# Computing the first head group's values, queries and keys side by side in a two-layer hybrid trunk

## The chip, the cores and the metric

The kernel runs on one core of one Trainium2 chip. The metric is the device time in microseconds (us) of the whole program, taken over several executions. One execution is profiled; its trace gives the start and length of the instructions on each engine: TensorE (PE) for matmuls, VectorE (DVE), ScalarE (ACT), GpSimd (POOL) and SyncE (SP), which issues DMAs here.

## What is computed

A trunk of two layers over 256 positions and a model width of 2048, all in float32. Each layer is

```python
h = _rmsnorm(x, attn_norm[l])
z = jnp.einsum('bsd,dc->bsc', h, w_in[l])
(fq, fk, fv, fg, mq, mk, mv, dq, dk, dv, sq, sk, sv) = _split_cols(z)
fox = _forgetting_attention(...)       # gate fg + b_fgate, cumulative log-sigmoid
moba = _moba_attention(...)            # rotary positions on q and k
diff = _differential_attention(...)    # rotary, difference of two softmaxes, norm
sb = _stick_breaking_attention(...)    # log-sigmoid of scores, cumulated from the right
mixed = jnp.concatenate([...], axis=-1)
x = x + jnp.einsum('bsc,cd->bsd', mixed, w_out[l])
h = _rmsnorm(x, ffn_norm[l])
act = jax.nn.silu(h @ w_gate[l]) * (h @ w_up[l])
x = x + act @ w_down[l]
```

with four heads of 128 in each of the four groups (a product of one group and one of q, k, v is 2048 x 512), a feed-forward width of 5632, and a last RMSNorm. The `rmsnorm` is applied late: products are taken of x times the norm's gain, and the factor of each row (`rcol`) is multiplied in when a product is read out of PSUM.

## The kernel before

**Blocks.** All weights stream from memory as blocks of 128 x 1024 floats (512 KB). An "in" product (2048 x 512) is 8 blocks, each with two chunks of 128 rows. A layer has 96 "in" blocks, then 32 "out", 176 "ffn" and 88 "down" blocks; layer 1 begins at block 392. `ORDER` is diff, moba, sb, fox. `load` (L186) issues a block's DMA on SP's queue into one of four buffers (`raw`). `split_parts` rounds it on ACT to `hi` (L195) and takes the rest on DVE as `lo` (L196), three buffers of each. `rows_block` does the block's 12 matmuls of 128 x 512 on PE (L356 to L358: hi with x's lo, lo with x's hi, hi with x's hi, for two chunks and two halves of the positions). x is likewise kept in halves `xh` (L299 on ACT, L300 on DVE), 16 chunks.

**Order.** All engines work through queues in the order in which the program writes the instructions. `rows_block(b)` first calls `run_ahead(b)`, which splits block b+2 and issues loads up to block b+5, then writes the matmuls of b, then calls `tick`, which lets three queues of generators do one step each: `evacs` (reading products out of PSUM and turning them), `background` (the steps of attention of a group, after its q and k are ready) and `spare` (the gate of fox). A step's instructions so stand between the work of one block and the next. `drain(evacs)` does all that is left of that queue at once. The buffers of `hi` are such that hi of block n waits for PE's end of block n-3.

**Products.** Each "in" product has two PSUM tiles of the pool's tag "mm", which has four; small pieces take the four of the tag "at". Rotary products are read by four multiplies on DVE (`z` and `ms`, L415), two sums, two transposes (L384); `mem` is written by a DMA (L387) and read back by four (L393). Products without rotary are read by two copies on ACT (L425 for q and k, L815 for v).

**The start.** In layer 0, x comes two chunks with each of blocks 1 to 7, ahead of the block's load (`beside`); its chunks are squared on ACT, added on POOL, and `attn_norm_steps` makes `rcol` from the sum: a table load and Ln, a table load and Exp on ACT (L305, L306), four small operations on DVE (L307 to L310). In layer 1, x's chunks come out of the last down products (`add_turned`), four at a time.

**The first group.** diff has v, then q, then k, each 8 blocks; the other groups q, k, v. The gate's steps (`gate_steps`, spare) wait for 50 ticks of the layer, then do one step a tick: 32 sums `gacc` (L518 on DVE, half of them on POOL) and 16 small matmuls `pf` (L530) that stand ahead of block 84. Stick-breaking's chain: scores, exponentials, a table load and Ln on ACT (L707, L708), `n` on DVE (L711 to L715), its halves `h` on ACT (L720) and `l` on DVE (L721), and the updates of its scores on PE.

Of the kernel before, what the change touches and what calls it, by code (L numbers as in the profile page):

```python
# [11 lines left out]
F32 = mybir.dt.float32  # L12
# [7 lines left out]
P = 128  # L20
# [7 lines left out]
NJ = D // P  # L28
FFN = 5632
NF = FFN // P  # L30
GC = 512
# [6 lines left out]
ORDER = ("diff", "moba", "sb", "fox")  # L38
# [12 lines left out]
def columns(name, which):  # L51


    c0 = COL0[name] + "qkv".index(which) * GW
    order = np.arange(GW)
    if which != "v":
        order = order.reshape(NH, 4, 32).transpose(1, 0, 2).reshape(-1)
    return c0 + order
# [9 lines left out]
C_KEEP = C_SL + P  # L68
# [36 lines left out]
def lay_out(inp):  # L105

    pd, pf = turned(D), turned(FFN)
    x_t = np.ascontiguousarray(inp["x"][0].T[pd].reshape(NJ, P, S).transpose(1, 0, 2))
    vec = np.zeros((P, V_ALL), np.float32)
    blocks = np.empty((sum(n for _, _, n in plan()), P, 1024), np.float32)  # L110
    at = 0

    def put(w, rows, cols, wide):
        nonlocal at
        m = w[rows][:, cols] if not isinstance(cols, slice) else w[rows, cols]
        k = 1024 // wide
        nb = m.shape[0] // (k * P)
        blocks[at:at + nb] = m.reshape(nb, k, P, wide).transpose(0, 2, 1, 3).reshape(nb, P, 1024)
        at += nb

    for l in range(DEPTH):
        w_in, every = inp["w_in"][l][pd], slice(None)
        v = vec[:, l * V_LAYER:(l + 1) * V_LAYER]
        v[:, V_GA:V_GA + 16] = inp["attn_norm"][l][pd].reshape(16, P).T
        v[:, V_GF:V_GF + 16] = inp["ffn_norm"][l][pd].reshape(16, P).T
        v[:, V_WF:V_WF + 64] = w_in[:, FG0:FG0 + NH].reshape(16, P, NH).transpose(1, 0, 2).reshape(P, 64)
        v[:, V_SUB] = inp["diff_subln"][l]
        v[:, V_B:V_B + NH] = inp["b_fgate"][l]
        for n, name in enumerate(("diff_lq1", "diff_lk1", "diff_lq2", "diff_lk2")):
            v[:, V_LAM + 64 * n:V_LAM + 64 * (n + 1)] = inp[name][l]  # L130
        for kind, what, nb in plan():
            if what[0] != l:
                continue
            if kind == "in":
                put(w_in, every, columns(*what[1:]), GC)
            elif kind == "out":
                order = np.concatenate([HEAD0[g] * P + np.arange(GW) for g in ORDER])
                put(inp["w_out"][l], order[what[2] * 256:what[2] * 256 + 256], np.arange(what[1] * GC, what[1] * GC + GC), GC)
            elif kind == "ffn":
                c = slice(what[1] * GC, what[1] * GC + GC)  # L140
                for n, name in enumerate(("w_gate", "w_up")):
                    blocks[at:at + NJ, :, n * GC:n * GC + GC] = inp[name][l][:, c][pd].reshape(NJ, P, GC)
                at += NJ
            else:
                put(inp["w_down"][l], pf, slice(what[1] * GC, what[1] * GC + GC), GC)
    fin = np.ascontiguousarray(np.broadcast_to(inp["final_norm"], (P, D)))
    return {"x_t": x_t, "vec": vec, "w": blocks, "consts": constants(), "fin": fin}
# [7 lines left out]
def plan():  # L155

    out = []
    for l in range(DEPTH):
        for g in ORDER:
            out += [("in", (l, g, which), 8) for which in ("vqk" if g == ORDER[0] else "qkv")]  # L160
        out += [("out", (l, c, kb), 1) for c, kb in OUT_ORDER]
        out += [("ffn", (l, c), NJ) for c in range(NFC)]
        out += [("down", (l, c), NFC * 2) for c in range(4)]
    return out
# [3 lines left out]
def trunk(ctx: ExitStack, tc: tile.TileContext, x_t, vec, w, consts, fin, y):  # L168
# [39 lines left out]
    con = cp.tile([P, C_KEEP], F32, name="con")  # L208
    con_in = big.tile([P, C_ALL - C_KEEP], F32, name="con_in", tag="t13")
    nc.scalar.dma_start(vecs[:, :V_GF], vec[:, :V_GF])  # L210
    beside = {b: [(x_all[:, 2 * b:2 * b + 2], x_t[:, 2 * b:2 * b + 2])] for b in range(1, NJ // 2)}
    for b, (to, of, c0, c1) in enumerate([(con, consts, C_ID, C_KEEP), (con, consts, 1024, C_ID), (con, consts, 0, 1024),
                                          (vecs, vec, V_GF, V_ALL)]):
        beside[NJ // 2 + b] = [(to[:, c0:c1], of[:, c0:c1])]
    beside[NJ // 2 + 4] = [(con_in, consts[:, C_KEEP:])]
    raws[0] = wp.tile([P, 1024], F32, name="raw0", tag="raw", bufs=RAW)
    for j in range(2):
        nc.sync.dma_start(xs[j], x_t[:, j])
# [3 lines left out]
    def run_ahead(b):  # L222
        nonlocal loaded, done_split
        while done_split < min(b + SPLIT, n_blocks):
            while loaded < min(done_split + RAW, n_blocks):
                for to, of in beside.get(loaded, ()):
                    nc.sync.dma_start(to, of)
                load(loaded)
                loaded += 1
            if done_split < NJ // 2:  # L230
                parts = split_parts(done_split, 1 if done_split else 2)
                for j in range(2 * done_split, 2 * done_split + 2):
                    halves_of_x(j, vcol(0, V_GA + j))
                    next(parts, None)
                for _ in parts:
                    pass
            else:
                split(done_split)
            done_split += 1
# [38 lines left out]
    def drain(queue):  # L278
        while queue:
            step(queue)  # L280
# [461 lines left out]
    STEPS = {"fox": fox_steps, "moba": moba_steps, "diff": diff_steps, "sb": sb_steps}  # L742

    def setup_steps():
        while loaded < 16:
            yield
        V.tensor_copy(id_bf, ident)
        V.tensor_copy(mq_bf, con_in[:, C_MQ - C_KEEP:C_MQ - C_KEEP + P])
        V.tensor_copy(mk_bf, con_in[:, C_MK - C_KEEP:C_MK - C_KEEP + P])
        A.activation(con_r[:, :3], con_in[:, :3 * P].rearrange("p (n c) -> p n c", n=3), AF.Copy)  # L750
        A.activation(one_r, cst(C_ONE), AF.Copy)
        yield
        e = tp.tile([P, DEPTH, 2], F32, name="le", tag="le", bufs=1)
        for l in range(DEPTH):
            lv = vcol(l, V_LAM, 256).rearrange("p (a b d) -> p a b d", a=2, b=2)
            pr = tp.tile([P, 2, 64], F32, name="pr", tag="pr", bufs=1)
            V.tensor_tensor(pr, lv[:, :, 0], lv[:, :, 1], op=ALU.mult)
            V.tensor_reduce(e[:, l], pr, axis=AX, op=ALU.add)
        yield
        A.activation(e, e, AF.Exp)  # L760
        yield
        for l in range(DEPTH):
            init = 0.8 - 0.6 * math.exp(-0.3 * l)
            nl = cp.tile([P, 1], F32, name=f"nlam{l}")
            V.tensor_tensor(nl, e[:, l, 1:2], e[:, l, 0:1], op=ALU.subtract)
            V.tensor_scalar(nl, nl, -init, None, op0=ALU.add)
            state["nlam", l] = nl
            gs = cp.tile([P, 1], F32, name=f"gsub{l}")
            V.tensor_scalar(gs, vcol(l, V_SUB), 1.0 - init, None, op0=ALU.mult)
            state["gsub", l] = gs  # L770
        yield

    def first_squares():
        for j in range(NJ):
            square_sum(j)
            if j % 2:
                yield

    def attention(l):
        if l == 0:  # L780
            evacs.append(first_squares())
        evacs.append(attn_norm_steps(l))
        for n, name in enumerate(ORDER):
            at = 3 * (n % 2)
            qk = {which: tmp(at + i, [P, NH, S], which) for i, which in enumerate("qk")}
            vt = tmp(at + 2, [P, 2, GW], "v")
            ready = {}

            def v_part():
                outs = in_product()  # L790
                if n:
                    drain(evacs)
                evacs.append(v_steps(vt, outs, ready))
                if n:
                    drain(evacs)

            def pairs():
                for which in "qk":
                    evacs.append(q_or_k_steps(name, which, in_product(), qk[which], ready))

            if n == 0:
                if l == 0:
                    background.append(setup_steps())
                spare.append(gate_steps(l))
                v_part()
                pairs()
                background.append(group_steps(l, name, qk, ready))
            else:
                pairs()
                background.append(group_steps(l, name, qk, ready))  # L810
                v_part()

    def v_steps(vt, outs, ready):
        for t in range(2):
            A.activation(vt[:, t], outs[t], AF.Copy, scale=state["rcol"][:, t:t + 1])  # L815
        ready["v"] = vt
        yield
# [189 lines left out]
```

## Time and profile before

| | before |
|---|---|
| median of 3 runs | 2247.93 us (2247.28 to 2248.83) |
| the profiled execution | 2248.83 us |
| its span, first to last instruction | 2247.0 us |
| PE busy | 2223.6 us (99%) |
| DVE busy | 1301.0 us (58%) |
| ACT busy | 1054.6 us (47%) |
| POOL busy | 195.8 us (9%) |
| DMA, mean over the span | 212 GB/s |

A row of a timeline gives the start in us from the span's start, the time of the row's instructions, engine, line, operation, the tiles written and read with their shape, and how many followed one another (x2: the time is that of both). In brackets stand the engine's idle time just before and the instruction that ended it. The granted clock of PE is 1.00 at 2.4 GHz and 0.5 at 1.2 GHz; a table by windows gives its mean in each. Matmuls are pipelined: a row's time is longer than the step to the next one.

### The profile page before, as it was taken

The page shows a single profiled execution, that of the slowest core. Times are in us where ns is not written, and L with a number is a line of the kernel's source. Part 1 is how long each engine was busy: PE and PEld are TensorE (multiplying, and loading weights), DVE is VectorE, ACT ScalarE, POOL GpSimd, SP SyncE. Part 2 cuts the span into 40 slices and gives each one's busy share as a digit, 9 for nine tenths or more (in the row PEclk, how much of TensorE's full clock was granted, in tenths as well). Part 3 has the DMA queues.
Part 4 walks back from the last instruction along what each step waited for, and adds up shares of the span by engine and source line. Part 5 has one row for each costly group of instructions (what it writes and reads, how often), then busy time and mean ns, then how long its engine had stood idle before and what let it go on. Part 6 is the DMA issues. An engine that isn't in the chain of part 4 may idle for free.

```text
span 2247.0 us, 26619 instructions
## 1 busy us (share of the span) xinstructions
PE 2223.6 (99%) x9977; PEld 1832.2 (82%) x9977; DVE 1301.0 (58%) x1442; ACT 1054.6 (47%) x1296; POOL 195.8 (9%) x189
## 2 busy tenths in 40 slices
PE   9999999999999999999999999999999999999997
PEld 6888888788888888888878888878888888888886
DVE  6768655655555555455566776566555555554444
ACT  6454644544444444444444556445444444444443
POOL 2019200100000000000000290011000000000000
PEclk9999999999999999999999999999999999999999
DMA  7766556777667667666657565567777776676664
GB/s 256 225 206 203 181 188 206 231 223 216 215 217 227 209 212 226 213 207 206 209 196 232 191 203 188 183 214 228 226 223 237 250 231 211 224 223 199 201 196 147
DMA packets 190497, 476.42 MB, mean 212 GB/s; under 512 B 17440, under 2 KB 72992, under 8 KB 190368
## 3 DMA queue, kind: packets, MB, share of 16 engines
q1 hardware_dynamic: 189792, 473.93, 66.2%
q8 instruction: 78, 1.28, 0.2%
q10 hardware_dynamic: 576, 0.79, 0.1%
q14 instruction: 51, 0.42, 0.1%
HBM read 444.24 MB, written 30.41 MB: 211 GB/s over the span
## 4 chain that ended last, share of the span: by engine, by line
PE 89%; DMA 4%; DVE 3%; ACT 2%; issue 1%; SPq 1%; ACTq 0%; DVEq 0%
PE gate L374 20%; PE up L374 20%; PE po L356 9%; PE po L358 9%; PE po L357 9%; PE in L356 7%; PE in L357 7%; PE in L358 7%; DMA back<-mem 2%; DMA mem<-tr 2%; DVE lo L196 1%; ACT hi L195 1%; SPq L393 0%; DVE x_all L833 0%; DVE tr L384 0%
## 5 line engine op out<-in xcount | busy, mean ns | idle before, releaser
L196 DVE TENSOR_TENSOR lo<-raw,hi 128x1024 fp32r<-128x1024 f32 (+1 forms) x785 | 961.2, 1227 | 880.1 <-ACT hi L195 879.6
L195 ACT ACTIVATE hi<-raw 128x1024 fp32r<-128x1024 f32 (+1 forms) x785 | 829.6, 1059 | 1080.3 <-PE up L374 487.4
L374 PE MATMUL gate<-hi,xh 128*128 128x512 f32 x1408 | 548.2, 389 | 0.5 <-ACT hi L195 0.5
L374 PE MATMUL up<-hi,xh 128*128 128x512 f32 x1408 | 547.8, 389 | 0.0
L374 PEld LDWEIGHTS gate<-hi,xh 128*128 128x128 f32 x1408 | 264.3, 188 | 56.0 <-ACT hi L195 1.2
L374 PEld LDWEIGHTS up<-hi,xh 128*128 128x128 f32 x1408 | 264.4, 188 | 54.8
L356 PE MATMUL in<-hi,xh 128*128 128x512 f32 x768 | 304.7, 397 | 4.1 <-ACT hi L195 2.3
L357 PE MATMUL in<-lo,xh 128*128 128x512 f32 x768 | 301.5, 393 | 1.4 <-DVE lo L196 1.3
L358 PE MATMUL in<-hi,xh 128*128 128x512 f32 x768 | 301.0, 392 | 0.0
L374 PE MATMUL gate<-lo,xh 128*128 128x512 f32 x704 | 274.5, 390 | 1.1 <-DVE lo L196 1.1
L374 PE MATMUL up<-lo,xh 128*128 128x512 f32 x704 | 273.9, 389 | 0.0
L356 PE MATMUL po<-hi,act 128*128 128x512 f32 x704 | 273.9, 389 | 0.0
L357 PE MATMUL po<-lo,act 128*128 128x512 f32 x704 | 273.9, 389 | 0.0
L358 PE MATMUL po<-hi,act 128*128 128x512 f32 x704 | 273.9, 389 | 0.0
L356 PEld LDWEIGHTS in<-hi,xh 128*128 128x128 f32 x768 | 145.4, 189 | 34.9 <-ACT hi L195 3.4
L357 PEld LDWEIGHTS in<-lo,xh 128*128 128x128 f32 x768 | 145.3, 189 | 32.5 <-DVE lo L196 3.3
L358 PEld LDWEIGHTS in<-hi,xh 128*128 128x128 f32 x768 | 145.3, 189 | 30.7
L374 PEld LDWEIGHTS gate<-lo,xh 128*128 128x128 f32 x704 | 132.1, 188 | 30.6 <-DVE lo L196 3.4
L358 PEld LDWEIGHTS po<-hi,act 128*128 128x128 f32 x704 | 132.2, 188 | 27.5
L357 PEld LDWEIGHTS po<-lo,act 128*128 128x128 f32 x704 | 132.2, 188 | 27.4
L356 PEld LDWEIGHTS po<-hi,act 128*128 128x128 f32 x704 | 132.2, 188 | 27.4
L374 PEld LDWEIGHTS up<-lo,xh 128*128 128x128 f32 x704 | 132.2, 188 | 27.2
(206 smaller groups left out, 1473.8 us busy)
## 6 DMA issues: line engine op xcount, KB each, us to landing
raw<-w SPq DMA_DIRECT2D x783, 512.0 KB, 4.3
mem<-tr SPq DMA_DIRECT2D x50, 512.0 KB, 4.3
back<-mem SPq DMA_DIRECT2D x168, 128.0 KB, 4.8
k<-mem SPq DMA_DIRECT2D x24, 128.0 KB, 4.2
memb<-trb SPq DMA_DIRECT2D x16, 128.0 KB, 3.8
x_all<-memb SPq DMA_DIRECT2D x4, 512.0 KB, 6.2
x_all<-x_t SPq DMA_DIRECT2D x7, 256.0 KB, 7.1
q<-mem SPq DMA_DIRECT2D x8, 128.0 KB, 4.7
```

The source lines that it names most:

```text
L195: A.activation(hi[:, c], raw[:, c], AF.Copy)
L196: V.tensor_tensor(lo[:, c], raw[:, c], hi[:, c].bitcast(F32), op=ALU.subtract)
L356: T.matmul(outs[t], xlo, wh, start=first, stop=False)
L357: T.matmul(outs[t], xhi, wl, start=False, stop=False)
L358: T.matmul(outs[t], xhi, wh, start=False, stop=last)
L374: T.matmul(outs[n][t], st, wt[:, n * GC:(n + 1) * GC], start=first, stop=last)
```

## The change

The weights of diff are laid out so that blocks come in the order v, q, k of the first two chunks of x, then v, q, k of the next two, and so on ("first"). `attention` opens all three products at once, k's on two PSUM tiles of the tag "at", and runs through the 24 blocks; then it drains `evacs`, reads v out, and queues the steps for q and k. This holds for both layers. In layer 0 the pairs of x's chunks are loaded, halved and squared with every third block in place of every block, the constants with blocks 4, 7, 10 and 13, `con_in` with 16, and the setup waits for 20 loads.

```diff
@@ plan
         for g in ORDER:
-            out += [("in", (l, g, which), 8) for which in ("vqk" if g == ORDER[0] else "qkv")]
+            if g == ORDER[0]:
+                out += [("first", (l, g, which, kb), 1) for kb in range(8) for which in "vqk"]
+            else:
+                out += [("in", (l, g, which), 8) for which in "qkv"]
@@ trunk
-    beside = {b: [(x_all[:, 2 * b:2 * b + 2], x_t[:, 2 * b:2 * b + 2])] for b in range(1, NJ // 2)}
+    beside = {3 * p: [(x_all[:, 2 * p:2 * p + 2], x_t[:, 2 * p:2 * p + 2])] for p in range(1, NJ // 2)}
...
-        beside[NJ // 2 + b] = [(to[:, c0:c1], of[:, c0:c1])]
-    beside[NJ // 2 + 4] = [(con_in, consts[:, C_KEEP:])]
+        beside[4 + 3 * b] = [(to[:, c0:c1], of[:, c0:c1])]
+    beside[16] = [(con_in, consts[:, C_KEEP:])]
@@ run_ahead
-            if done_split < NJ // 2:
+            if done_split < 3 * NJ // 2 and done_split % 3 == 0:
                 parts = split_parts(done_split, 1 if done_split else 2)
-                for j in range(2 * done_split, 2 * done_split + 2):
+                p = 2 * done_split // 3
+                for j in range(p, p + 2):
@@ setup_steps
-        while loaded < 16:
+        while loaded < 20:
@@ first_squares
-            if j % 2:
-                yield
+            if j % 2 and j + 1 < NJ:
+                for _ in range(3):
+                    yield
@@ attention
                 spare.append(gate_steps(l))
-                v_part()
-                pairs()
+                outs = {which: [ps.tile([P, GC], F32, name=f"in{t}", tag="at" if which == "k" else "mm") for t in range(2)]
+                        for which in "vqk"}
+                for kb in range(8):
+                    for which in "vqk":
+                        rows_block(x_source, outs[which], kb, 8)
+                drain(evacs)
+                evacs.append(v_steps(vt, outs["v"], ready))
+                step(evacs)
+                for which in "qk":
+                    evacs.append(q_or_k_steps(name, which, outs[which], qk[which], ready))
                 background.append(group_steps(l, name, qk, ready))
```

In the rows of order below, a name's first number belongs to the program where it counts blocks (hi25, lo84, raw53), and the number behind the underscore is a buffer's.

ACT at the norm of layer 0; `v_106` reads the two PSUM tiles of diff's v. Before, with hi of blocks 10 to 12 ahead:

```order
L195 ACTIVATE hi10_381<-raw10_297 128x1024
L195 ACTIVATE hi11_399<-raw11_328 128x1024
L195 ACTIVATE hi12_420<-raw12_353 128x1024
L305 ACT_TABLE_LOAD
L305 ACTIVATE isq_439<-v_436 128x2
L306 ACT_TABLE_LOAD
L306 ACTIVATE isq_439<-isq_439 128x2
L815 ACTIVATE v_106<-in0_107,rcol_438 128x512
```

After, at the same place:

```order
L200 ACTIVATE hi24_658<-raw24_590 128x1024
L200 ACTIVATE hi25_679<-raw25_614 128x1024
L311 ACT_TABLE_LOAD
L311 ACTIVATE isq_698<-v_695 128x2
L312 ACT_TABLE_LOAD
L312 ACTIVATE isq_698<-isq_698 128x2
L830 ACTIVATE v_106<-in0_107,rcol_697 128x512
L830 ACTIVATE v_106<-in1_108,rcol_697 128x512
```

The norm and the reading of v have moved from behind hi of block 12 to behind hi of block 25.

DVE around `n` and `l` of stick-breaking, with the gate's sums `gacc` between (tr: fox's q, turned). Before:

```order
L196 TENSOR_TENSOR lo77_2123<-raw77_2047,hi77_2122 128x1024
L711 SCALAR_TENSOR_TENSOR n0_2021<-z0_2025,e0_2019 128x512
L711 SCALAR_TENSOR_TENSOR n0_2021<-z1_2028,e0_2019 128x512
L712 SCALAR_TENSOR_TENSOR n1_2022<-z1_2031,e1_2020 128x512
L714 TENSOR_TENSOR n0_2021<-n0_2021,con_76 128x4x128
L715 TENSOR_TENSOR n1_2022<-n1_2022,con_76 128x512
L518 SCALAR_TENSOR_TENSOR gacc_1422<-x_all_75,wf_1423,gacc_1422 128x256
L196 TENSOR_TENSOR lo78_2150<-raw78_2072,hi78_2149 128x1024
L721 TENSOR_TENSOR l0_2167<-n0_2021,h0_2165 128x1024
L721 TENSOR_TENSOR l1_2168<-n1_2022,h1_2166 128x512
L518 SCALAR_TENSOR_TENSOR gacc_1422<-x_all_75,wf_1423,gacc_1422 128x256
L196 TENSOR_TENSOR lo79_2180<-raw79_2096,hi79_2179 128x1024
```

After:

```order
L201 TENSOR_TENSOR lo83_2260<-raw83_2179,hi83_2259 128x1024
L390 STREAM_TRANSPOSE tr_2275<-z_2248 128x512 x2
L717 SCALAR_TENSOR_TENSOR n0_2160<-z0_2164,e0_2158 128x512
L717 SCALAR_TENSOR_TENSOR n0_2160<-z1_2167,e0_2158 128x512
L718 SCALAR_TENSOR_TENSOR n1_2161<-z1_2170,e1_2159 128x512
L720 TENSOR_TENSOR n0_2160<-n0_2160,con_76 128x4x128
L721 TENSOR_TENSOR n1_2161<-n1_2161,con_76 128x512
L524 SCALAR_TENSOR_TENSOR gacc_1372<-x_all_75,wf_1373,gacc_1372 128x256
L201 TENSOR_TENSOR lo84_2290<-raw84_2204,hi84_2289 128x1024
L727 TENSOR_TENSOR l0_2309<-n0_2160,h0_2307 128x1024
L727 TENSOR_TENSOR l1_2310<-n1_2161,h1_2308 128x512
L524 SCALAR_TENSOR_TENSOR gacc_1372<-x_all_75,wf_1373,gacc_1372 128x256
```

The chain stands six blocks later, with the two transposes in it, and the gacc in its last row is now the last of the gate's sums, the one that pf reads.

SP's queue at the turning of moba's k (`k_729` before, `k_710` after). Before:

```order
L186 DMA raw48_1215<-w 128x1024
L387 DMA mem_1233<-tr_1205 128x2x512
L186 DMA raw49_1240<-w 128x1024
L186 DMA raw50_1262<-w 128x1024
L393 DMA k_729<-mem_1233 32x8x128 x4
L186 DMA raw51_1294<-w 128x1024
```

After:

```order
L191 DMA raw51_1218<-w 128x1024
L191 DMA raw52_1245<-w 128x1024
L393 DMA mem_1276<-tr_1273 128x2x512
L399 DMA k_710<-mem_1276 32x8x128 x4
L191 DMA raw53_1289<-w 128x1024
L191 DMA raw54_1319<-w 128x1024
```

The two weight loads between the write of mem and its four reads are gone, and raw53 stands behind the reads.

## Rows read from the trace of the kernel before

**Rows 1.** Page, part 1: busy us (share of the span) x instructions, one engine.

```profile
PE 2223.6 (99%) x9977; PEld 1832.2 (82%) x9977; DVE 1301.0 (58%) x1442; ACT 1054.6 (47%) x1296; POOL 195.8 (9%) x189
```

**Rows 2.** Waits of PE: engine line, waited for: us in total, times, longest.

```profile
PE in L356 <- ACT hi L195: 2.3, 2, 2.0
```

**Rows 3.** Table by windows: us, busy time of each engine, granted clock, DMA share, GB/s.

```profile
10.00:20.00 10.00, 8.17 (x22) 6.27 (x23) 8.79 (x11) 9.13 (x18) 3.26 (x4) 0.66 1.03 399
...
1140.00:1150.00 10.00, 9.66 (x35) 7.82 (x36) 6.38 (x7) 5.26 (x10) 3.33 (x4) 0.83 0.40 135
```

**Rows 4.** Timeline of PE, blocks 1 and 13.

```profile
11.07 0.50 PE L356 MATMUL in<-hi,xh 128*128 128x512 f32 x1 [1.96 <-ACT hi L195]
...
12.33 0.79 PE L357 MATMUL in<-lo,xh 128*128 128x512 f32 x1 [0.76 <-DVE lo L196]
...
48.81 0.50 PE L357 MATMUL in<-lo,xh 128*128 128x512 f32 x1 [0.29 <-DVE lo L196]
```

**Rows 5.** Timeline of PE, start of layer 1.

```profile
1138.06 0.39 PE L358 MATMUL in<-hi,xh 128*128 128x512 f32 x1
...
1140.34 0.50 PE L356 MATMUL in<-hi,xh 128*128 128x512 f32 x1 [1.89 <-DVE xh L300]
```

**Rows 6.** Timeline of ACT, start of layer 0.

```profile
8.55 0.51 ACT L299 ACTIVATE xh<-x_all,vecs 128x256 fp32r<-128x256 f32 x1 [1.65 <-DMA x_all<-x_t]
...
9.96 1.06 ACT L195 ACTIVATE hi<-raw 128x1024 fp32r<-128x1024 f32 x1 [0.91 <-DMA raw<-w]
```

**Rows 7.** Timeline of ACT, the norm of layer 0.

```profile
39.71 1.06 ACT L195 ACTIVATE hi<-raw 128x1024 fp32r<-128x1024 f32 x1 [1.67 <-PE in L358]
...
40.78 1.28 ACT L305 ACT_TABLE_LOAD   x1
...
44.67 1.27 ACT L815 ACTIVATE v<-in,rcol 128x512 f32<-128x512 f32 x2 [0.82 <-DVE rcol L310]
```

**Rows 8.** Timeline of DVE, multiplies of diff's k.

```profile
102.83 1.40 DVE L415 SCALAR_TENSOR_TENSOR z<-in,rcol,con 128x512 f32<-128x512 f32 x2
```

**Rows 9.** Timeline of PE, scores of diff ahead of block 32.

```profile
100.49 1.15 PE L612 MATMUL s<-k,q 64*128 64x128 f32 x8
...
101.78 0.47 PE L356 MATMUL in<-hi,xh 128*128 128x512 f32 x1
```

**Rows 10.** Page, part 6: DMA issues, KB each, median us to landing.

```profile
raw<-w SPq DMA_DIRECT2D x783, 512.0 KB, 4.3
...
mem<-tr SPq DMA_DIRECT2D x50, 512.0 KB, 4.3
...
k<-mem SPq DMA_DIRECT2D x24, 128.0 KB, 4.2
```

**Rows 11.** Timelines of ACT and DVE, start of layer 1.

```profile
1124.89 1.06 ACT L195 ACTIVATE hi<-raw 128x1024 fp32r<-128x1024 f32 x1 [1.66 <-PE in L358]
...
1124.41 1.30 DVE L384 STREAM_TRANSPOSE tr<-po 128x512 f32<-128x512 f32 x2
```

**Rows 12.** Timeline of ACT, stick-breaking's chain, and later fox's q.

```profile
236.35 1.06 ACT L195 ACTIVATE hi<-raw 128x1024 fp32r<-128x1024 f32 x1 [0.19 <-PE in L358]
...
237.43 1.28 ACT L707 ACT_TABLE_LOAD   x1
...
256.25 1.25 ACT L425 ACTIVATE z<-in,rq 128x512 f32<-128x512 f32 x2
```

**Rows 13.** Timeline of DVE, stick-breaking's chain.

```profile
241.29 1.23 DVE L196 TENSOR_TENSOR lo<-raw,hi 128x1024 fp32r<-128x1024 f32 x1 [2.22 <-ACT hi L195]
...
242.43 1.28 DVE L711 SCALAR_TENSOR_TENSOR n<-z,e 128x512 f32<-128x512 f32 x2
...
245.82 1.22 DVE L196 TENSOR_TENSOR lo<-raw,hi 128x1024 fp32r<-128x1024 f32 x1
...
248.70 0.48 DVE L518 SCALAR_TENSOR_TENSOR gacc<-x_all,wf,gacc 128x256 f32<-128x256 f32 x1
```

**Rows 14.** Timeline of PE, start of block 78.

```profile
247.03 0.39 PE L356 MATMUL in<-hi,xh 128*128 128x512 f32 x1
```

More of the change, by code (lines that the diff above doesn't have):

```diff
@@ L135, in lay_out @@
                 put(w_in, every, columns(*what[1:]), GC)
+            elif kind == "first":
+                put(w_in, slice(what[3] * 256, what[3] * 256 + 256), columns(*what[1:3]), GC)
             elif kind == "out":
```

## The prediction

> **What bounds the kernel now.** I read the page's first part, then what TensorE (PE) waits for, then the timelines of the stretches that the change touches, engine by engine. PE is busy for 2223.6 of 2247.0 us [rows 1]: at full clock a block of 12 matmuls takes 2.72 us, and everything else in the kernel has to hide under that. Only some 23 us of the span are not PE time, and most of them are ramp and tail, so little can be gained and a good deal can be lost. The waits say the same: the largest line is 2.3 us in all [rows 2]. The thing to look for is therefore what has so far been hidden with little to spare, and where the change moves it.
>
> The waits that do exist are at two places. At the start, PE has finished block 0, waits for hi of block 1, does one matmul at 11.07 and waits again for lo until 12.33; the granted clock over 10 to 20 us is 0.66 [rows 3, 4]. With levels of 1.0 and 0.5 that is (1-0.66)/0.5*10 = 6.8 us at half clock, which cost 3.4 us. In layer 1, PE waits from 1138.06 to 1140.34 for the halves of x chunk 12, and the clock over 1140 to 1150 is 0.83, that is 3.4 us at half clock, 1.7 us lost [rows 3, 5]. So an idle of some 2 us was followed by half clock twice, with a price of 1.7 to 3.4 us on top of the idle.
>
> **Part 1, the start.** In before, the load of x chunks 2 and 3 stands ahead of block 1's weights; they land at 8.53 and 9.94, seen by the xh and the hi that they release [rows 6]. In after, blocks 1 and 2 use chunks 0 and 1 again, and the load of x 2-3 comes behind w1 and w2. 1024 KB had landed at 8.53 and 1536 KB at 9.94; after's w1 completes 1280 KB, so by interpolation 9.2, an estimate between those two rows. PE resumes 0.7 us earlier. If the half-clock stretch is then as long as layer 1's (3.4 us) rather than 6.8, another 1.7 comes back, less some 0.4 for the two pauses around the single matmul. I take -2.0; bounds -0.5 (only the earlier landing, partly lost) and -4.5 (clock not lowered at all). The lo wait at 48.1 (0.68 between starts in place of 0.23, [rows 4]) goes with the x loads that made it: -0.45.
>
> **Part 2, the values behind the norm (block 24, layer 0).** In before, diff's v is finished at block 7 and its PSUM pair is wanted again only at block 16; the norm and the evacuation, which end about 45 us, are covered. In after, v is finished at block 21 to 23, and moba's q at block 24 takes v's pair at once. The order of ACT there is hi25, table load, Ln, table load, Exp, then v. In before the same sequence ran from 39.71 (hi, released by the end of a block) to the start of v at 44.67, with a first copy of some 0.68 (two in 1.27) [rows 7]: 45.35 - 39.71 = 5.64 us from the end of block 22. PE has only block 23 to do, 2.72 us. Idle: 5.64 - 2.72 = 2.9, say 3.0 with the start of a waiting matmul. That is longer than both idles of [rows 4, 5], so half clock follows: +1.7 (nearest: layer 1's case, where PE then ran on without a pause), bounds 0 and 3.4. Together +4.7. In layer 1 nothing of the norm is left on ACT there: v ends about 1.9 us after block 414, under block 415; 0.
>
> A rule bears on this chain. Rows 7 show 4.96 us between the start of hi and that of v, which two loads of 1.28, hi of 1.06, two tiny activations and some 0.8 on DVE fill. The Trainium skill, ScalarE: Activation LUTs, section "What ACT_TABLE_LOAD costs", gives 1.28 us for the load and a drain of about 1.38 us with it at every switch. By that page block 24 would wait 2.8 us longer and each pf 1.4, and the sum would be 2270.9. The trace leaves no room for such a drain, so I don't add it.
>
> **Part 3, evacuations that queue up.** The steps for q and k of diff now begin after block 23 instead of 15 and 23, so moba's q waits in the queue: its table multiplies (four, 0.7 each [rows 8]) are given out only after block 39, behind lo41, and moba's v wants that bank at block 40. The third of the four ends 1.06+1.23+3*0.7 = 4.4 us after the end of block 38; PE is there after 2.72 + 1.3 for the diff scores, which now stand ahead of block 40 [rows 9], = 4.0. About 0.4 in each layer: +0.8. At block 48 sb's q waits for the two copies of moba's v, 0.3 in each layer, +0.6, bounds 0 and 0.7 (one copy, [rows 7]).
>
> **Part 4, moba's k at block 47.** `drain` now meets the whole of moba's k: on SP the write of mem and the four reads of k stand directly behind one another, and raw53 behind them; in before two weight loads stand between. SP waits for mem to land with all weight loads behind it. Counted from the end of block 46: lo49 done at 2.3, multiplies 2.8, two sums and a copy some 1.7 (an estimate: a sum as long as a multiply), transposes 1.3, mem 4.3, four issues some 1.8, raw53 4.3 [rows 8, 10, 11]: 18.5, hi53 at 19.6, lo53 at 20.8. PE wants block 53 after six blocks and two groups of scores [rows 9], 16.3 + 2.7 = 19.0, and its lo 0.2 later: 1.6 late. The softmax scaling that then stands on DVE adds perhaps 0.6. +2.2 a layer, +4.4; bounds 0 (mem lands sooner) and 3.5 a layer.
>
> **Part 5, layer 1's start.** Chunks 12 to 15 of x are now wanted at the 19th block of the layer instead of the 7th, so the wait of 2.28 - 0.23 = 2.05 and its 1.7 of half clock go: -3.75 (bounds -3.0, -5). The second block, q, now takes a pair that the last down product leaves: the first of its two transposes ends at 1124.41 + 0.7 = 1125.1, while the block could start at the end of the one before, some 0.2 ahead of the hi at 1124.89 which that end released [rows 11]: +0.45.
>
> **Part 6, block 84, the largest term.** The diff group is complete as late as before, but its attention steps begin eight blocks later, and all groups' steps behind it shift. Stick-breaking's scores move from before block 72 to before 78, while the gate's 32 steps are counted from the layer's start and do not move: pf still stands ahead of block 84 and wants the last gacc. In before it waits for nothing (pf is in no line of the waits). In after, the stick-breaking chain lies just ahead of it, together with fox's q: on ACT hi82, two z copies, table load, Ln, hi83; on DVE lo83, two transposes, n, gacc, lo84, l, gacc. In before's times (block 78 of before for block 84 of after) hi starts at 236.35 and the last gacc of that stretch ends at 248.70 + 0.48 = 249.18 [rows 12, 13]. ACT gets 1.25 more ahead of hi83 (the two z copies, [rows 12]), DVE some 1.25 more for the two transposes (1.30, [rows 11]): 251.7. PE comes to pf at 247.03 [rows 14]. lo78 was done there at 245.82 + 1.22 = 247.04 [rows 13], just in time, so there is no reserve at all. Idle 251.7 - 247.03 = 4.6, with half clock behind it +1.7 (bounds 0 and 3.4): 6.3 a layer, +12.6.
>
> **Sum.** -2.0 - 0.45 + 4.7 + 0.8 + 0.6 + 4.4 - 3.75 + 0.45 + 12.6 = +17.35. Against the profiled execution, 2248.83 + 17.35 = 2266.2; that execution is 0.9 above the median of its runs, 2247.93, so 2265.3 for the median.
>
> **Rivals.** *Everything stays hidden* (the other side): ACT and DVE are busy for 47% and 58% of the span only, and if the evacuations at blocks 24, 48 and 84 find the engines free, only the gains remain: -2.0 - 0.45 - 3.75 + 0.45 = -5.75, 2242. It decides at 84: the chain would have to end at 247.0 instead of 251.7. Against it stands the order of the queues, in which each of these steps is behind another that cannot start early. *Block 84 alone is free*, because earlier waits of PE let DVE get ahead: 2265.3 - 12.6 = 2252.7. Against it: hi is tied to the end of the block three before, so a wait of PE moves the splits too. *The clock pays more*: half clock of 6.8 instead of 3.4 us after blocks 24, 84 and 476: +5.1, 2270.4. *The change does not do what it says* at the start, w1 landing as late as 9.94: +1.5, 2266.8, within the forecast's own spread.
>
> **How the numbers follow.** Forecast 0.76, everything hidden 0.04, block 84 free 0.12, clock pays more 0.08. About 0.2% or 4.5 us is what a measurement of this kernel can tell from no change: same is 2243.4 to 2252.4. Everything hidden gives faster 0.03 and 0.01 of same; block 84 free lies on the upper edge, 0.06 same and 0.06 slower; the rest is slower: 0.03, 0.07, 0.90. The range goes down to block 84 free, 2253, and up to the upper bounds of parts 2, 4 and 6 together, 2265.3 + 1.7 + 2.6 + 3.4 = 2273, with 2 more for waits that no row shows: 2275.
>
> **What would show it.** In the profile of the changed kernel: PE resuming for block 1 near 11.6 and full clock near 15; an idle of 3.0 on PE ended by ACT v in layer 0 and none in layer 1; no wait for xh at layer 1's start; `pf` waiting 4 to 5 us for DVE gacc in each layer, the largest line of the waits; raw53 landing late. The prediction is wrong if pf does not wait, or if half clock is not seen behind these idles (then 2260).

## The result: slower by 0.95%

The changed kernel takes 2271.18 us in the median of four runs (2268.76 to 2272.26), the kernel before 2248.38 (2247.28 to 2249.98, four runs); the ratio is 1.0095, with a 95% interval of 1.0082 to 1.0108. Forecast was 2265.3, in 2253 to 2275. The profiled execution of the changed kernel took 2268.76, the shortest of its four, with a span of 2267.0; the one of before 2248.83. So the traces explain 19.9 of the 22.8 us between the medians.

The page of the changed kernel and the head of what PE waits for (in all, times, longest), which answer to [rows 1] and [rows 2]:

```profile
PE 2230.1 (98%) x9977; PEld 1837.9 (81%) x9977; DVE 1303.7 (58%) x1442; ACT 1054.3 (47%) x1296; POOL 204.5 (9%) x189
```

```profile
PE pf L536 <- DVE gacc L524: 8.0, 4, 2.8
PE in L363 <- DVE lo L201: 3.4, 5, 1.1
PE in L362 <- ACT v L830: 2.6, 1, 2.6
PE po L362 <- ACT hi L200: 1.7, 2, 0.9
PE po L363 <- DVE lo L201: 1.5, 2, 0.8
PE s L618 <- DMA k<-mem: 1.4, 2, 0.8
```

The same matmuls are done; PE is busy for 6.5 us more, POOL for 8.7, and the other engines differ by less than 6 us. What is new is in the list: `pf` waiting for the gate's sums is now the largest wait, and v of diff and the scores' reads of k, which were 0.2 before, stand in it. The wait for `xh` at the start of layer 1 (1.9) is gone.

Where the time went is read from the start of the same block on PE in both traces:

| start of block | before | after | difference |
|---|---|---|---|
| 4 | 23.18 | 19.20 | -3.98 |
| 23 | 75.92 | 71.25 | -4.67 |
| 25 | 81.36 | 79.69 | -1.67 |
| 48 | 150.72 | 149.26 | -1.47 (+3.0 = +1.5) |
| 83 | 265.88 | 264.08 | -1.80 (+5.0 = +3.2) |
| 88 | 281.32 | 292.05 | +10.73 |
| 392 | 1121.97 | 1133.94 | +11.97 |
| 400 | 1147.52 | 1156.37 | +8.85 |
| 440 | 1264.28 | 1270.10 | +5.82 (+3.0 = +8.8) |
| 475 | 1379.45 | 1384.53 | +5.08 (+5.0 = +10.1) |
| 480 | 1394.90 | 1413.66 | +18.76 |
| 783 | 2232.88 | 2252.80 | +19.92 |

The numbers in brackets add the small matmuls of attention that the kernel before had done by that block and the changed one had not. They are read from blocks of the kernel before that took longer than 2.72 us with no wait in them (0.9 + 1.5 + 0.6 up to block 48, 2.5 + 2.5 between 78 and 81).

**Block 24.** ACT in the changed kernel (start, length, line, operation), and PE at the start of block 24:

```profile
71.09 1.06 ACT L200 ACTIVATE hi<-raw 128x1024 fp32r<-128x1024 f32 x1 [1.67 <-PE in L364]
72.17 1.28 ACT L311 ACT_TABLE_LOAD   x1
73.51 0.20 ACT L311 ACTIVATE isq<-v 128x2 f32<-128x2 f32 x1
73.73 1.28 ACT L312 ACT_TABLE_LOAD   x1
75.02 0.20 ACT L312 ACTIVATE isq<-isq 128x2 f32<-128x2 f32 x1
76.05 1.26 ACT L830 ACTIVATE v<-in,rcol 128x512 f32<-128x512 f32 x2 [0.82 <-DVE rcol L316]
```

```profile
76.79 0.50 PE L362 MATMUL in<-hi,xh 128*128 128x512 f32 x1 [2.56 <-ACT v L830]
```

The chain of [rows 7] stands here unchanged, 4.96 us from hi to v, and PE waits through 2.7 us of it. Ln begins 0.06 us after the load's end: the drain of 1.38 us that the Trainium skill (ScalarE: Activation LUTs, What ACT_TABLE_LOAD costs) adds to each switch is not seen here either.

**Block 84.** DVE and PE in the changed kernel, with the instructions of [rows 13]:

```profile
262.21 1.23 DVE L201 TENSOR_TENSOR lo<-raw,hi 128x1024 fp32r<-128x1024 f32 x1 [3.37 <-ACT hi L200]
263.35 1.30 DVE L390 STREAM_TRANSPOSE tr<-z 128x512 f32<-128x512 f32 x2
264.57 1.25 DVE L717 SCALAR_TENSOR_TENSOR n<-z,e 128x512 f32<-128x512 f32 x2
...
267.53 0.48 DVE L524 SCALAR_TENSOR_TENSOR gacc<-x_all,wf,gacc 128x256 f32<-128x256 f32 x1
267.93 1.22 DVE L201 TENSOR_TENSOR lo<-raw,hi 128x1024 fp32r<-128x1024 f32 x1
269.06 1.82 DVE L727 TENSOR_TENSOR l<-n,h 128x1024 fp32r<-128x1024 f32 x2
270.80 0.48 DVE L524 SCALAR_TENSOR_TENSOR gacc<-x_all,wf,gacc 128x256 f32<-128x256 f32 x1
```

```profile
268.16 0.35 PE L536 MATMUL pf<-con,gacc 128*128 128x1 f32 x2 [1.19 <-DVE gacc L524]
271.33 3.15 PE L536 MATMUL pf<-con,gacc 128*128 128x1 f32 x14 [2.83 <-DVE gacc L524]
274.34 0.77 PE L362 MATMUL in<-hi,xh 128*128 128x512 f32 x1
```

From lo83 to the last gacc DVE has no gap: 262.21 to 271.28, nine microseconds of queue in which PE can do only what was already split. PE waits twice, 4.0 us together, and the clock falls. By windows (us, busy times, granted clock, DMA share, GB/s), around pf in layer 0 and in layer 1:

```profile
264.00:284.00 20.00, 15.98 (x73) 12.98 (x72) 11.55 (x20) 10.58 (x14) 0.00 (x0) 0.83 0.61 184
1385.00:1405.00 20.00, 15.98 (x67) 12.93 (x66) 10.99 (x19) 10.58 (x14) 0.00 (x0) 0.74 0.59 180
```

That is (1-0.83)/0.5*20 = 6.8 and, from 0.74, 10.4 us at half clock. In layer 1 the clock is at half (0.50) from 1390.4 to 1391.7 already, while PE still waits, and that part of the stretch slows no matmul. By the table of blocks the two places cost 7.5 and 8.7 us (from 83 to 88: 10.73 - 3.2; from 475 to 480: 18.76 - 10.1), so the clock took 3.5 and 4.7 on top of each 4.0.

### The profile page after: what moved, and what is told of

It reads as the page before. It is cut to its first block, busy times and chain, and to the rows that moved or that the text cites. A ratio compares the mean times of both kernels' runs of the same rounds, so it can differ in the third digit from the quotient of the medians.

```text
span 2267.0 us, 26625 instructions
## 1 busy us (share of the span) xinstructions
PE 2230.1 (98%) x9977; PEld 1837.9 (81%) x9977; DVE 1303.7 (58%) x1442; ACT 1054.3 (47%) x1296; POOL 204.5 (9%) x189
## 4 chain that ended last, share of the span: by engine, by line
PE 86%; DVE 5%; DMA 4%; ACT 3%; issue 2%; SPq 1%; ACTq 0%; DVEq 0%
PE up L380 20%; PE gate L380 20%; PE po L362 9%; PE po L363 9%; PE po L364 9%; PE in L362 6%; PE in L363 6%; PE in L364 6%; DMA mem<-tr 2%; DVE lo L201 1%; ACT hi L200 1%; DMA back<-mem 1%; DMA raw<-w 1%; DVE tr L390 1%; SPq L399 1%
## 5 line engine op out<-in xcount | busy, mean ns | idle before, releaser
L301 POOL TENSOR_TENSOR acc<-acc,sq 128x256 f32<-128x256 f32 x60 | 54.3, 904 | 1137.0 <-ACT sq L300 1134.8
```

Of the source, the lines that this page charges most:

```text
L301: G.tensor_tensor(state["acc"], state["acc"], sq, op=ALU.add)
```

## The experiments

Each kernel ran beside the kernel before on the same chip; a ratio is against that, with its 95% interval. The kernel before had medians of 2248.5 (e1 to e4), 2249.2 (e5 to e8) and 2247.5 us (e9 and e10) in the three groups against 2248.38 in the changed kernel's own, so a difference to the changed kernel's 2271.18 carries up to 0.8 us from the groups.

### e1_pf_later: pf three blocks later

```diff
@@ gate_steps
+        for _ in range(3):
+            yield
         state["gate", l] = yield from gate_end_steps(l, acc)
```

> The changed kernel with one edit: the gate lets three ticks pass between its last gacc and the pf matmuls, so pf stands ahead of block 87 instead of 84; nothing else moves. Theory 'place of pf': PE's idle at block 84 is due only to where pf stands. Then the 4.0 us of idle and the 3.4 to 5.1 us lost at half clock behind it go in both layers, 15 to 18 us off the changed kernel's 2271. Theory 'DVE is behind': lo of block 84 ends at 269.15 in the changed kernel's trace while PE could begin it at 266.8, so block 84 waits 2.1 us for lo instead, and only 2 us of idle a layer go, with whatever the clock then does: 4 us off if it still falls as long, up to 13 if it does not fall.

Measured: 2258.97 us, ratio 1.0050 (1.0032 to 1.0068), 12 us below the changed kernel. pf waits no more, and block 84 waits for lo in its stead:

```profile
267.56 0.50 PE L363 MATMUL in<-lo,xh 128*128 128x512 f32 x1 [2.01 <-DVE lo L201]
```

So the theory "DVE is behind" holds in its place and size, 2.0 us where 2.1 were expected, in both layers. The time came out near that theory's upper end: half clock behind this shorter idle was 0 in layer 0 and 3.4 us in layer 1. Moving pf took away one of two waits and most of the clock's price, but not the cause.

### e2_gate_58: the whole gate eight blocks later

```diff
@@ gate_steps
-        for _ in range(50):
+        for _ in range(58):
             yield
```

> The changed kernel with the gate's steps counted from 58 ticks instead of 50, so that gacc and pf move eight blocks later, as diff's attention has. Theory 'place of pf': 15 to 18 us off, as with pf alone. Theory 'DVE is behind': gacc still takes 0.48 us of every block there, so block 84 waits 2.1 us for lo, as with pf alone; beside that the gate's sums no longer lie on diff's softmax scaling, and the waits of 0.6 and 1.1 us at block 56 shrink by about a microsecond in each layer.

Measured: 2257.47 us, ratio 1.0040 (1.0026 to 1.0055). The same wait for lo at block 84, 2.0 us in each layer:

```profile
PE in L363 <- DVE lo L201: 4.8, 3, 2.0
PE in L362 <- ACT v L830: 2.6, 1, 2.6
```

The lo waits are 4.8 in all against e1's 7.2: the waits at block 56 (up to 0.8 for p and 1.1 for lo in e1) are gone from both layers. The time is 13.7 us below the changed kernel, and by the intervals it can't be told from e1's. So the second part of part 4's cost, too, was the gate's sums lying on another chain.

### e3_x_half_pace: x every second block

```diff
-    beside = {3 * p: [(x_all[:, 2 * p:2 * p + 2], x_t[:, 2 * p:2 * p + 2])] for p in range(1, NJ // 2)}
+    beside = {2 * p: [(x_all[:, 2 * p:2 * p + 2], x_t[:, 2 * p:2 * p + 2])] for p in range(1, NJ // 2)}
...
-        beside[4 + 3 * b] = [(to[:, c0:c1], of[:, c0:c1])]
+        beside[(5, 9, 13, 15)[b]] = [(to[:, c0:c1], of[:, c0:c1])]
@@ first_squares
-                for _ in range(3):
+                for _ in range(2):
```

> The changed kernel with x loaded and squared two chunks every second block instead of every third; the constants go with odd blocks. The norm then stands some seven blocks earlier. Theory 'the norm makes v late': the 2.7 us of idle at block 24 of layer 0 goes and the start stays within 0.5 us of the changed kernel's, 2.7 us off. Rival 'v is late because its bank is wanted at once, norm or not': the wait shrinks to what two copies cost, 0.7 to 1.3 us, 1.5 to 2 us off. Second rival, the loads of x now compete with the first weights: the start gives back up to 2 us and nothing is gained.

Measured: 2264.42 us, ratio 1.0076 (1.0058 to 1.0094). No wait for v is left in the trace, block 24 starts at 74.09 instead of 76.79, 2.7 earlier, and block 4 at 19.22 instead of 19.20. It was the norm, and the slow pace of x bought nothing at the start that the half pace doesn't. The median is 6.8 us below the changed kernel where 2.7 were expected; the ratios differ by 0.0019, some 4 us, and their intervals overlap, so the 2.7 rest on the trace and not on the time.

### e4_layer1_plain: layer 1 as before the change

```diff
@@ plan
-            if g == ORDER[0]:
+            if g == ORDER[0] and l == 0:
                 out += [("first", (l, g, which, kb), 1) for kb in range(8) for which in "vqk"]
             else:
-                out += [("in", (l, g, which), 8) for which in "qkv"]
+                out += [("in", (l, g, which), 8) for which in ("vqk" if g == ORDER[0] else "qkv")]
@@ attention
+                if l:
+                    v_part()
+                    pairs()
+                    background.append(group_steps(l, name, qk, ready))
+                    continue
```

> The changed kernel with layer 1 as it was before the change (v, then q, then k of diff), layer 0 as changed. By the two traces layer 1 took 1133.1 us in the changed kernel against 1125.1 us, so about 8 us should come off, with the wait for xh of chunk 12 (2.05 us) and its half clock back, and no wait of pf in layer 1. Rival 'what layer 1 loses is only the phase of the clock': less than 4 us off.

Measured: 2263.73 us, ratio 1.0068 (1.0052 to 1.0085), 7.4 below the changed kernel, as expected. Its waits show pf in one layer (4.0 in two waits) and the wait for xh back (1.9). So in the changed kernel layer 1 has the loss of block 84 as layer 0 has it (+8.7 in the table), and its gain at the layer's start (-3.1) doesn't pay for that.

### e8_x23_first: the old place of the first x load

```diff
-    beside = {3 * p: [(x_all[:, 2 * p:2 * p + 2], x_t[:, 2 * p:2 * p + 2])] for p in range(1, NJ // 2)}
+    beside = {3 * p if p > 1 else 1: [(x_all[:, 2 * p:2 * p + 2], x_t[:, 2 * p:2 * p + 2])] for p in range(1, NJ // 2)}
```

> The changed kernel with one edit: the load of x chunks 2 and 3 stands ahead of block 1's weights again, as in the kernel before. Theory 'the start's gain is block 1's earlier weights': block 1's second matmul goes back from 8.5 us to 11 to 12.3 us, with an idle of about 2 us ahead of it, and block 4 starts 2 to 4 us later than the 19.2 of the changed kernel. Rival 'the gain is that fewer x loads lie between the first weights': block 1 loses under 1 us, block 4 starts within 1 us of 19.2.

Measured: 2275.41 us in its one run, which is too little to compare the time with the changed kernel's; only the start is read here. The 8.5 us in the expectation was a misreading: the matmul at 8.49 in the changed kernel is the second half of block 0, and block 1 goes on at 11.13. Block 1 on PE, of the changed kernel and then of this one:

```profile
9.87 0.49 PE L362 MATMUL in<-hi,xh 128*128 128x512 f32 x1
11.13 0.50 PE L363 MATMUL in<-lo,xh 128*128 128x512 f32 x1 [0.77 <-DVE lo L201]
```

```profile
10.66 0.51 PE L362 MATMUL in<-hi,xh 128*128 128x512 f32 x1 [0.72 <-ACT hi L200]
11.93 0.51 PE L363 MATMUL in<-lo,xh 128*128 128x512 f32 x1 [0.76 <-DVE lo L201]
```

Block 1 is 0.8 us later, within the rival's 1 us, but block 4 starts at 21.62 instead of 19.20, 2.4 later, as the first theory has it. Between the two lies the clock: over 10 to 20 us it is 0.83 here, that is 3.4 us at half clock and 1.7 lost, and 1.00 in the changed kernel. So between these two traces w1's earlier place is worth 2.4 of the 4.0 us gained at the start, most of it through the clock. That the other 1.6 come from the x loads that no longer lie between the first weights is likely, but was not tested.

### e5_repair: the three places mended together

```diff
@@ gate_steps
-        for _ in range(50):
+        for _ in range(58):
             yield
@@ sb_steps
         yield
+        yield
         A.activation(e0, e0, AF.Ln, bias=1.0)
```

and the edits of e3_x_half_pace.

> The changed kernel with three edits: x at two chunks every second block, the gate counted from 58 ticks, and stick-breaking's Ln one tick later, so that n no longer stands directly behind the transposes of fox's q on DVE. Theory 'DVE is behind because two chains meet in one tick': the lo wait of 2.0 us at block 84, which the gate's move alone left, goes in both layers, and so does the wait of 2.7 at block 24; 2257.5 of the gate's move alone less 4.0 less 2.7, less up to 3.4 of half clock: 2247 to 2251, no different from the kernel before. Rival 'the eight-block shift costs elsewhere as soon as this place is mended': lo or pf waits of 1 to 2 us appear a block or two later and it stays above 2254.

Measured: 2245.76 us, ratio 0.9989 (0.9978 to 1.0001). Neither pf nor v is in the list of waits, and the lo waits are 1.0 in all. So the loss of 23 us was at these places; the time is even a little below the 2247 to 2251 of the expectation. Beside e2, where only the gate was moved and lo still waited 2.0 us, the tick ahead of Ln is the one edit here that bears on block 84; it was not run alone. DVE now has `n` directly behind lo, with no transposes between:

```profile
257.50 1.23 DVE L201 TENSOR_TENSOR lo<-raw,hi 128x1024 fp32r<-128x1024 f32 x1 [0.72 <-ACT hi L200]
258.64 1.28 DVE L718 SCALAR_TENSOR_TENSOR n<-z,e 128x512 f32<-128x512 f32 x2
...
262.04 1.22 DVE L201 TENSOR_TENSOR lo<-raw,hi 128x1024 fp32r<-128x1024 f32 x1
```

```profile
263.47 0.39 PE L363 MATMUL in<-lo,xh 128*128 128x512 f32 x1
```

The second lo ends at 262.04 + 1.22 = 263.26, and PE's matmul with it starts on time at 263.47. One tick is enough for DVE to keep up with the gate moved as well, but only by 0.2 us.

### e7_repair_layer1_plain: the repair without layer 1's interleaving

This is e5_repair with the edits of e4_layer1_plain.

> The kernel e5_repair with layer 1's first group as before the change. Theory 'once the chains are apart, interleaving in layer 1 pays what part 5 says': the wait for xh of chunk 12 (2.05 us) and its half clock (1.7 us) come back, the wait of 0.57 at the layer's second block goes: 3 us above e5_repair. Rival 'interleaving layer 1 still costs through the eight-block shift': e7 is 1 to 4 us below e5_repair. The gate's place (58 instead of 50) is new for a plain layer and may itself move layer 1 by a microsecond or two either way.

Measured: 2246.64 us, ratio 0.9987 (0.9977 to 0.9998), against 0.9989 (0.9978 to 1.0001) for e5_repair. The two can't be told apart. By its trace layer 1's wait for xh is back (1.9), but 3 us were expected and none can be measured: whether interleaving layer 1 pays at all stays open.

### e6_repair_scores_later: diff's reading queue one tick longer

```diff
@@ q_or_k_steps
+            if name == "diff":
+                yield
         ready[which] = True
```

> The kernel e5_repair with one more edit: diff's scores are given out one tick later, so that they don't wait on PE for the reads of k from memory (0.7 to 2.0 us in the traces so far, in one layer or both). Theory 'the scores come too early for the reads': that wait goes and nothing else comes, 1 to 2 us off e5_repair, and up to 1.7 more where the clock fell behind it. Rival 'the reads are late because the queue is full': the wait moves with the scores or shows as a raw that lands late, no change.

Measured: 2260.12 us, ratio 1.0049 (1.0031 to 1.0067), 14 us above e5_repair; neither theory. The empty tick stands in the queue that also reads moba's q, and moba's v wants that bank at block 40:

```profile
121.99 0.76 PE L362 MATMUL in<-hi,xh 128*128 128x512 f32 x1 [4.47 <-DVE ms L421]
```

In layer 0 and in layer 1 PE waits 4.5 us for the multiplies that were given out one block later, and the trace has another 1.2 in each at block 48. The wait for the reads of k is not in this trace.

### e9_scores_alone_later: the scores later, the reading where it was

```diff
@@ group_steps
             yield
+        if name == "diff":
+            for _ in range(1):
+                yield
         yield from STEPS[name](l, *(by_heads(name, which, qk[which]) for which in "qk"), ready)
```

> The kernel e5_repair with diff's attention steps one tick later, given out from their own queue, so that the reading of moba's q (which e6_repair_scores_later also put off by a tick, at 4.5 us a layer) stays where it is. Theory 'the scores come too early for the reads of k': the wait of the scores on the reads (1.0 us in e5_repair's trace, up to 2 in others) goes in both layers and nothing else comes: 1 to 2 us below e5_repair's ratio, about 0.998 of the kernel before. Rival 'the reads are late because the queue is full': no change against e5_repair, 0.999.

Measured: 2248.01 us, ratio 0.9994 (0.9985 to 1.0003): no gain on e5_repair. The wait of the scores is gone, and in its place stands

```profile
119.80 0.47 PE L362 MATMUL in<-hi,xh 128*128 128x512 f32 x1 [2.30 <-DVE ms L421]
```

The scores had been doing something useful ahead of block 40: they filled 1.3 us of the time in which PE would otherwise wait for ms. The first theory's wait went and brought no time. No change is what the rival forecast, but the reads, which take 7.4 to 7.8 us in layer 0 here, are no longer what PE waits for: one wait was traded for another.

### e10_moba_q_earlier: one tick out of the reading queue

```diff
@@ turn_steps
-    def turn_steps(get, back=None):
+    def turn_steps(get, back=None, short=False):
...
         yield
-        yield
+        if not short:
+            yield
         return back.rearrange("p a k n -> p k a n")
@@ q_or_k_steps, the case of k of diff
+                                  name == "diff")
@@ group_steps
+        if name == "diff":
+            for _ in range(2):
+                yield
```

on top of e5_repair.

> The kernel e9_scores_alone_later with the steps of diff's k one empty tick shorter, so that every reading of a product behind it starts a block earlier, with the scores where e9 has them. Theory 'one tick in this queue is worth a block of 2.72 us to whoever needs the bank': the wait of block 40 for ms (0.4 us) goes, with reserve, and moba's k is read and sent off a block earlier, away from the loads behind block 47; 0.5 to 1.5 us below e9. Rival 'the wait has reserve neither way': the chains meet at another place, up to 5 us above e9.

Measured: 2242.88 us, ratio 0.9976 (0.9967 to 0.9985), 4.7 us below the kernel before beside it and 5.1 below e9, where 0.5 to 1.5 were expected. The theory is right in its place, but the expectation put the wait for ms at 0.4 us, which is e5_repair's; e9 waits 4.1 for it in both layers together. Neither s nor ms nor v nor pf is in its waits, which begin with:

```profile
PE in L363 <- DVE lo L201: 2.0, 5, 0.8
PE po L362 <- ACT hi L200: 1.6, 2, 1.4
PE gate L380 <- DVE lo L201: 1.6, 3, 0.5
PE po L363 <- DVE lo L201: 1.5, 2, 0.8
```

So a tick either way in that queue decides 4.5 us of waiting a layer at block 40, and the change had put it on the wrong side by a few tenths (0.7 us for ms in its layer 1).

Where e10 is ahead of the kernel before can be read from its block starts: 4.6 us at block 24 (74.02 against 78.64), 2.2 at block 392, 5.3 at block 400 and 6.0 at block 783. The gains lie at the two places where interleaving was to gain, the start and layer 1's start (parts 1 and 5). The kernel before with the same shifts but without interleaving was not run, so how much of the 4.7 us the shifts alone would give stays open.

## Why the prediction held, point by point

The sum forecast +17.35 for the profiled execution; its trace shows +19.9. By parts, from the table of blocks above:

| part | forecast | measured |
|---|---|---|
| 1, start up to block 23 | -2.45 | -4.67 |
| 2, block 24 | +4.7 | +3.0 |
| 3, blocks 25 to 48, layer 0 / 1 | +0.7 / +0.7 | +3.2 / 0.0 |
| 4, blocks 48 to 83, layer 0 / 1 | +2.2 / +2.2 | +1.7 / +1.3 |
| 5, layer 1's start | -3.3 | -3.1 |
| 6, block 84, layer 0 / 1 | +6.3 / +6.3 | +7.5 / +8.7 |
| out, ffn and down, layer 0 / 1 | 0 / 0 | +1.2 / +1.2 |

The mechanism and the ranking of the places are right: block 84 is the largest term, forecast as 12.6 of the loss and measured as 16.2. That the sum came within 2.6 us is partly luck: the parts that came out lower than forecast miss by some 6 us together, those that came out higher by some 8.7, and the two nearly cancel. One sign that the prediction set itself held in part only: half clock was seen behind block 84 in both layers, but not behind block 24.

**Part 6 was right in place, mechanism and idle.** 4.6 us of idle were forecast from the rows of another place in the kernel, and 4.0 were waited, in two pieces. The term is under-sized by the clock: 1.7 us were put down for it, and 3.5 and 4.7 were paid, the second beyond the bound of 3.4. That DVE's queue, not the place of pf, is the cause is shown by e1 and e2, where pf is moved and lo waits 2.0 us at the same block, and by e5, where the queue is mended and PE no longer waits there.

**Part 2 was right in the wait and wrong in the clock.** 2.7 us of idle (2.95 between two starts, less the usual 0.23) where 2.9 to 3.0 were forecast; e3 shows the norm as its cause. The 1.7 of half clock behind it did not come in this execution.

**Part 1 was short by 2.2 us.** Its step on the landing was right but small: w1 releases hi of block 1 at 8.76, where 9.2 was interpolated, and block 1 goes on at 11.13 instead of 12.33, 1.2 us earlier where 0.7 was expected. ACT's hi of block 1 and the window of 10 to 20 us in the changed kernel:

```profile
8.76 1.06 ACT L200 ACTIVATE hi<-raw 128x1024 fp32r<-128x1024 f32 x1 [1.04 <-DMA raw<-w]
```

```profile
10.00:20.00 10.00, 9.23 (x40) 7.42 (x41) 8.07 (x8) 7.24 (x12) 2.90 (x3) 1.00 0.95 346
```

The larger error is the clock: PE's pauses there are now 0.1 and 1.0 us instead of 2.1 and 1.0, and the granted clock from 10 to 20 us is 1.00 where [rows 3] has 0.66. That end was put down as the bound, -4.5, and not as the value.

**Part 3 missed a wait.** In layer 1, block 40's place (432) waits 0.7 us for ms (0.4 forecast) and block 48's 0.25 for v (0.3 forecast), against small losses of the kernel before in the same stretch, so that nothing is left of them. In layer 0 block 48 waits the same 0.25. But the scores that stand ahead of block 40 waited for the reads of k, and the clock fell behind that, 3.4 us of matmuls at half pace from about 124:

```profile
121.22 0.46 PE L618 MATMUL s<-k,q 64*128 64x128 f32 x2 [0.57 <-DMA k<-mem]
122.52 0.68 PE L618 MATMUL s<-k,q 64*128 64x128 f32 x6 [0.84 <-DMA k<-mem]
```

In the kernel before these scores waited 0.2 us for the same reads in layer 1, so this place had no reserve either; the prediction looked at what the scores cover and not at what they need. In layer 0 of the changed kernel the four reads took 6.4 to 6.9 us from issue to landing, in the kernel before 3.7 to 4.5; in layer 1, where the scores didn't wait, 5.4 to 5.7 against 4.1 to 5.0. Why the reads are slower was not tested.

**Part 4 was near in size and only partly in place.** No wait at block 53 is in the trace; 0.6 for p in layer 0 and 0.3 in layer 1, with 1.1 for lo in each, come at block 56, where the softmax scaling and the gate's sums lie on one another. The four reads did stand at once behind mem, and the loads behind them landed late (raw53 at 163.0, 4.7 us after its issue at 158.3), but they were still in time.

**Part 5 was right** to 0.2 us in both pieces: +0.6 for the wait on the transposes of the last product, -3.8 for xh and the clock.

**Out, ffn and down** were not in the sum. The waits for hi and lo in the last out product (block 125 and its place in layer 1), which exist in the kernel before as well, grew by 1.2 in layer 0 (from 0.8 to 2.0); in layer 1 they grew by 0.5, and half clock behind them cost some 1.6 us, against 0.8 of small losses of the kernel before that no longer follow. Why they grew was not tested.

Of the rivals, "the clock pays more" (2270.4) came nearest, and it names the term that was too small, although block 24 went the other way. "Block 84 alone is free" and "everything hidden" are refuted by the list of waits; e10 reaches the time of the second (2242.9 against 2242), but only by moving the instructions apart.

## What to carry to other kernels

When work is moved by a number of blocks in a kernel whose queues are written out by hand, whatever is counted from another origin does not move with it. Lay the two against one another, tick by tick, and add up the engine's work between two splits; here two transposes in the same tick as `n` were enough for 2.0 us of waiting a layer. A matmul that stands ahead of the block is cover as well as cost, so before it is moved, look at what waits behind it, as e9 shows. And a change that loses 1% may hold a gain: the same interleaving with five steps shifted is 0.24% faster than the kernel before, though the shifts were not tried without it.

## What the runs showed of the hardware

The same idle doesn't always have the same price. In five traces PE waits the same 2.72 us at block 24 for v, and the granted clock around it differs. By windows from 70 to 90 us, the changed kernel, e1, e2 and e4:

```profile
70.00:90.00 20.00, 17.44 (x79) 14.17 (x78) 13.31 (x21) 10.49 (x12) 0.00 (x0) 1.00 0.51 167
```

```profile
70.00:90.00 20.00, 17.44 (x80) 14.12 (x79) 13.31 (x21) 10.50 (x12) 0.00 (x0) 1.00 0.50 165
```

```profile
70.00:90.00 20.00, 17.44 (x65) 13.87 (x65) 12.08 (x19) 9.61 (x12) 0.00 (x0) 0.83 0.43 144
```

```profile
70.00:90.00 20.00, 17.44 (x72) 13.96 (x71) 13.01 (x20) 9.54 (x12) 0.00 (x0) 0.91 0.45 159
```

PE is busy for 17.44 us in all four; the clock was at full speed throughout in two (and in e8, the fifth), and at half for (1-0.83)/0.5*20 = 6.8 and 3.6 us in the others. The two waits of pf, 4.0 us with a pair of tiny matmuls between, came with half clock at all seven places that have them (two each in the changed kernel, e3 and e8, one in e4), 6.8 or, by the rounded 0.74, 10.4 us of it. So in these traces the clock's price behind an idle of two to three microseconds doesn't follow from the idle's length, and belongs into the range of a forecast rather than into its sum. Whether it is also why runs of one kernel differ is only partly on record. The four runs of e1 took 2256.46, 2264.18, 2261.47 and 2256.22 us at mean granted clocks of 0.997, 0.994, 0.996 and 0.997: the lower the clock, the longer the run. The four of the changed kernel lie within 3.5 us, at 0.993, 0.992, 0.993 and 0.994, and show no such order.
